# An encoder block's branch A: transposed probabilities kept for four tiles, values' products of 512 columns, gate projections dealt out by the tile's place in its four

## The chip, the cores and the metric

The kernel runs on one core of a Trainium2 chip. The metric is the device time of one execution in microseconds; before the change it is 1440.57 us, the median of 3 runs (1439.94 to 1441.64).

## What is computed

One block of an encoder over 1024 tokens and 16 meta tokens that are put ahead of them, width 1024. Two attentions run beside each other on the same normed input: branch A, a differential attention over all 1040 positions (4 heads of 2 x 64 for the scores, 128 wide values), and branch B, a windowed attention. Their outputs are gated, summed, projected, and a feed-forward block follows. Branch A, which the change is about, is cut from the reference:

```python
s1 = jnp.einsum('bqhd,bkhd->bhqk', q1, k1).astype(jnp.float32) * scale + bias
s2 = jnp.einsum('bqhd,bkhd->bhqk', q2, k2).astype(jnp.float32) * scale + bias
attn = jax.nn.softmax(s1, axis=-1) - lam * jax.nn.softmax(s2, axis=-1)
return jnp.einsum('bhqk,bkhe->bqhe', attn.astype(v.dtype), v)
...
y = rms_norm(y, subln_g) * (1.0 - lambda_init)
```

The gates are projections of the same input (`sigmoid(h @ W)` for each branch, 1024 columns each), needed only after both branches are done.

## The kernel before, in words

Float32 products are made of three products of split numbers (hi x hi, hi x lo, lo x hi), so most operands exist as a hi and a lo part: ACT copies the hi part, DVE or POOL subtracts it to get lo (`split`, L113 and L114).

The program runs in stages: projections for both branches with branch B (to about 320 us), then branch A's attention (to about 617 us), then the branches' projections `ppa` (L589, from 630.52 us), the gated merge, and the feed-forward block. The stage of branch A is the one that changes:

- It loops over 4 heads x 8 tiles of 128 query rows, `n` = 0 to 31, with a lag of one tile: in turn `n` the scores of tile `n` are made and tile `n`-1 is transposed. `t` is the tile's number in its head.
- **Scores** (`scores_a`, L645): for the two halves `m` = 1, 0, three chunks of 352, 352 and 336 keys, each two products into one PSUM bank `aps`. DVE reduces each chunk (L651), ACT takes the exponential of a half (L656), POOL scales half 1 (L659), DVE joins the halves (L662), POOL copies 32 columns (L663).
- **Transposes** (`transpose_a`, L674): 9 blocks of a tile in three parts (4, 4 and 1 blocks), each part into one bank `apt`; ACT writes the hi part (L677) and DVE the lo part (L678) into `at`. Banks of `aps`, `apt`, and the small `apst` and `apf` come from one pool of 5 ("sc"); a bank is taken again when DVE (or ACT) has read what was in it.
- **Values** (`values_a`, L687): for each pair of tiles 25 products of 256 columns, in three parts of 9, 9 and 7, into half of the bank `apy` (ring "acc", one bank).
- **Norm** (`normed_a`): after both pairs of a four ACT reads `apy` (L694, L696), PE sums squares (`apst`, L700) and spreads the factor over the partitions (`apf`, L708), DVE multiplies (`yg`, L709), and SP stores 512 columns to `ya_d` (L710).
- **Gate projections**: 256 steps of three 512-column products each (`pp_g`, L209), 8 steps for a chunk of 512 tokens; ACT copies the finished chunk (L596), SP stores it to `g_d` (L597). They don't depend on the attention, and are put between its products as filler by `fill`.

PE's order is written out by hand: a string `SLOTS` (L40; `SLOTS_LAST`, L41, for the last head) says for each tile in which order a chunk of scores (s), a gate step (g), a part of the transposes (t) and a step of what waits in `tail` (n: values, then the norm's steps) are issued. The other engines' orders are decided when the kernel is built. After the last tile the loop at L779 empties `tail`, with three gate steps behind each step, and `fill(1000)` issues what gates are left.

The next stage starts with loads that SP issues behind the last stores: two weights `first_w` (L581, into `m0`) and four tiles of branch B's output, each in two halves (L843, `yb_d0` to `yb_d3` into `m1`), which are then split by ACT and DVE (L113, L114) and read by `ppa`, nine products of `yb0`, `yb1`, `yb2` ahead of the first three of `yb3`.

## Time and profile before

| what | value |
|---|---|
| median of 3 runs | 1440.57 us (1439.94 to 1441.64) |
| the profiled execution | 1440.88 us, its span 1438.9 us |
| mean granted clock of TensorE | 0.998 |
| PE busy | 1424.8 us, 99% of the span |
| DVE busy | 907.1 us, 63% |
| ACT busy | 672.7 us, 47% |
| POOL busy | 469.7 us, 33% |
| branch A: first scores, last `apf`, first `ppa` | 322.47, 616.88, 630.52 us |

The time of an execution is its span and about 2 us around it. PE's matmuls are pipelined: a row of the timeline gives the start of a group and the time to the end of its last one, and the next group starts before that. What an instruction costs on PE is therefore the distance between starts; its duration is longer.

### The profile page before, as it was taken

The page shows a single profiled execution, that of the slowest core. Times are in us where ns is not written, and L with a number is a line of the kernel's source. Part 1 is how long each engine was busy: PE and PEld are TensorE (multiplying, and loading weights), DVE is VectorE, ACT ScalarE, POOL GpSimd, SP SyncE. Part 2 cuts the span into 40 slices and gives each one's busy share as a digit, 9 for nine tenths or more (in the row PEclk, how much of TensorE's full clock was granted, in tenths as well). Part 3 has the DMA queues.
Part 4 walks back from the last instruction along what each step waited for, and adds up shares of the span by engine and source line. Part 5 has one row for each costly group of instructions (what it writes and reads, how often), then busy time and mean ns, then how long its engine had stood idle before and what let it go on. Part 6 is the DMA issues. An engine that isn't in the chain of part 4 may idle for free.

```text
span 1438.9 us, 20909 instructions
## 1 busy us (share of the span) xinstructions
PE 1424.8 (99%) x7279; PEld 1222.8 (85%) x7279; DVE 907.1 (63%) x1806; ACT 672.7 (47%) x1275; POOL 469.7 (33%) x462
## 2 busy tenths in 40 slices
PE   8999999999999999999999999999999999999998
PEld 6988899988898989888888888888888888888886
DVE  7356566428686868546887966645445553787566
ACT  6355555425454545455345754333333333444444
POOL 5143233223323232211503045555445552000442
PEclk9999999999999999999999999999999999999999
DMA  7334433481524252078341633433323333954444
GB/s 233 87 97 124 116 101 88 112 247 53 155 75 148 75 153 69 30 271 270 123 148 74 189 104 125 153 111 107 105 96 97 109 102 103 340 201 139 124 125 147
DMA packets 159051, 191.68 MB, mean 133 GB/s; under 512 B 16113, under 2 KB 103601, under 8 KB 158945
## 3 DMA queue, kind: packets, MB, share of 16 engines
q1 hardware_dynamic: 158368, 189.28, 42.0%
q8 instruction: 58, 0.95, 0.3%
q10 hardware_dynamic: 576, 1.05, 0.2%
q14 instruction: 49, 0.39, 0.1%
HBM read 129.80 MB, written 53.94 MB: 128 GB/s over the span
## 4 chain that ended last, share of the span: by engine, by line
PE 93%; DVE 2%; DMA 2%; ACT 1%; issue 1%; POOL 1%; SPq 0%; DVEq 0%; ACTq 0%
PE pg L1266 29%; PE pd L1370 13%; PE pp_g L209 12%; PE aps L645 4%; PE po L1169 4%; PE apy L687 3%; PE pp_ka L209 3%; PE pp_va L209 3%; PE pp_qb L209 3%; PE pp_qa L209 3%; PE ppa L589 3%; PE apt L674 2%; PE bps L333 2%; PE po L1177 2%; PE bpy L373 1%; PE bpt L368 1%
## 5 line engine op out<-in xcount | busy, mean ns | idle before, releaser
L1266 PE MATMUL pg<-t,wop 128*128 128x512 f32 x1056 | 242.4, 389 | 0.0
L1266 PEld LDWEIGHTS pg<-t,wop 128*128 128x128 f32 x1056 | 198.3, 188 | 41.1
L1370 PE MATMUL pd<-ob,oa 128*128 128x512 f32 x924 | 210.1, 389 | 0.2 <-DVE ob L114 0.2
L114 POOL TENSOR_TENSOR wop<-wf,wop 128x512 fp32r<-128x512 f32 x114 | 154.4, 1355 | 162.5 <-ACT wop L113 148.8
L1370 PEld LDWEIGHTS pd<-ob,oa 128*128 128x128 f32 x924 | 173.4, 188 | 36.7 <-DVE ob L114 0.5
L1266 PE MATMUL pg<-b,wop 128*128 128x512 f32 x792 | 183.3, 389 | 0.8 <-ACT c L1278 0.8
L1266 PEld LDWEIGHTS pg<-b,wop 128*128 128x128 f32 x792 | 148.5, 188 | 31.7 <-ACT c L1278 1.0
L114 POOL TENSOR_TENSOR wl_c<-w_c,wh_c 128x1024 fp32r<-128x1024 f32 x32 | 78.3, 2447 | 123.6 <-ACT wh_c L113 97.0
L113 ACT ACTIVATE wop<-wf 128x512 fp32r<-128x512 f32 x128 | 80.7, 632 | 74.2 <-PE pg L1266 45.9
L656 ACT ACTIVATE as<-as,amn 128x1040 f32<-128x1040 f32 x64 | 74.5, 1165 | 73.6 <-DVE amn L651 73.6
L209 PE MATMUL pp_g<-hT_hi,wh_c 128*128 128x512 f32 x256 | 101.3, 396 | 0.0
L209 PE MATMUL pp_g<-hT_hi,wl_c 128*128 128x512 f32 x256 | 100.9, 394 | 0.0
L209 PE MATMUL pp_g<-hT_lo,wh_c 128*128 128x512 f32 x256 | 100.9, 394 | 0.0
L113 ACT ACTIVATE oa<-ra 128x512 fp32r<-128x512 f32 x77 | 48.7, 632 | 108.9 <-PE pd L1370 50.2
L645 PE MATMUL aps<-ak,aq 128*128 128x352 f32 (+1 forms) x384 | 92.7, 326 | 0.0
L114 POOL TENSOR_TENSOR oa<-ra,oa 128x512 fp32r<-128x512 f32 x27 | 35.0, 1296 | 169.3 <-ACT oa L113 167.9
L1043 DVE TENSOR_TENSOR s<-wf,wf 128x512 f32<-128x512 f32 x22 | 15.6, 707 | 114.4 <-DMA wf<-in_w_ff_up_dram 62.8
L645 PEld LDWEIGHTS aps<-ak,aq 128*128 128x128 f32 x384 | 69.5, 188 | 14.2 <-issue 0.2
L651 DVE CUSTOM_DVE_ANT_0 as<-aps,dist,amn 128x352 f32<-128x352 f32 (+1 forms) x128 | 71.3, 563 | 10.4 <-PE aps L645 8.3
L345 POOL TENSOR_SCALAR bs<-bs,bdn 128x432 f32<-128x432 f32 (+1 forms) x64 | 37.2, 602 | 122.8 <-DVE bdn L343 92.6
L651 DVE CUSTOM_DVE_ANT_0 as<-aps,dist,far_a 128x352 f32<-128x352 f32 x64 | 37.1, 580 | 43.2 <-PE aps L645 43.0
L659 POOL TENSOR_SCALAR as<-as,adn,neglam 128x1040 f32<-128x1040 f32 x32 | 39.0, 1219 | 75.6 <-DVE adn L657 75.6
(283 smaller groups left out, 3050.6 us busy)
## 6 DMA issues: line engine op xcount, KB each, us to landing
ra<-aop SPq DMA_DIRECT2D x77, 256.0 KB, 2.7
w_c<-in_w_in_dram SPq DMA_DIRECT2D x33, 512.0 KB, 3.9
wf<-in_w_ff_gate_dram SPq DMA_DIRECT2D x25, 512.0 KB, 3.9
wf<-in_w_ff_up_dram SPq DMA_DIRECT2D x25, 512.0 KB, 3.8
aop<-as SPq DMA_DIRECT2D x44, 256.0 KB, 2.1
aop<-c SPq DMA_DIRECT2D x33, 256.0 KB, 2.0
g_d<-gate_stage SPq DMA_DIRECT2D x32, 256.0 KB, 2.0
gt<-g_d SPq DMA_DIRECT2D x32, 256.0 KB, 4.1
```

Source lines behind the costliest of these rows:

```text
L113: nc.scalar.activation(hi, src, AF.Copy)
L114: lo_eng.tensor_tensor(lo, src, f32(hi), ALU.subtract)
L209: nc.tensor.matmul(ps[:, :n], a[:, c, :], b[:, c, at:at + n], start=(c == 0 and i == 0), stop=(c == DC - 1 and i == 2))
L589: nc.tensor.matmul(ps, w[:, a, j, :], src(j, b, tk), start=(j == 0 and n == 0), stop=(j == 3 and n == 2))
L645: nc.tensor.matmul(ps[:, :n], qs[m][:, t * P:(t + 1) * P], ks[m][:, vv, k0:k0 + n], start=(vv == 0), stop=(vv == 1))
L651: nc.vector.tensor_tensor_reduce(s[m][:, a:b], ps[:, a - k0:b - k0], far_by, slope, low, ALU.add, ALU.min, mn[:, m, i + j:i + j + 1])
L656: nc.scalar.activation(s[m][:, 0:L], s[m][:, 0:L], AF.Exp, bias=low, scale=-1.0, accum_out=dn[:, m:m + 1])
L659: (nc.gpsimd if t % 4 in COMBINE_POOL else nc.vector).tensor_scalar(s[1][:, 0:L], s[1][:, 0:L], dn[:, 1:2], neglam, ALU.mult, ALU.mult)
L687: nc.tensor.matmul(py[:, cols], v[:kp, a, k, :], at_[:kp, k, b, :], start=(k == 0 and j == 0), stop=(k == 8))
L1169: nc.tensor.matmul(sets_o[p][u], oa[:, a, u * P:(u + 1) * P], ob[:, b, :], start=(p in (1, 5) and j == 0 and k == 0), stop=(p in (2, 3) an ...
L1266: nc.tensor.matmul(ps, op[:, x, c, :], b[:, y, c, :], start=(p in (1, 5) and c == 0 and n == 0), stop=(p in (4, 2, 3) and c == 3 and n == ...
L1370: nc.tensor.matmul(ps[u], oa[:, a, u * P:(u + 1) * P], ob[:, b, :], start=(p in (1, 2, 5) and j == 0 and k == 0), stop=(p in (2, 3, 4) and ...
```

## The change

The transposed probabilities of four tiles are kept in three tiles (`at0` and `at1` with 4 blocks each, `at2` with one; 2, 1 and 2 buffers), so that the values of a four are 25 products of 512 columns, 200 in all instead of 400 of 256 columns. They are issued in six parts, blocks (4, 5), (6, 7), 0, 1, 2, (3, 8), where there were three parts for each pair, and only after all four tiles are transposed. The norm follows directly. And the slots differ by `n` % 4: 7, 3, 4 and 6 gate steps for tile 0, 1, 2, 3 of a four (5 for each before), 6, 2, 3 and 5 in the last head (4 before).

```diff
-SLOTS = "sgsgsngsgsgstntnt"
-SLOTS_LAST = "sgsgsngsgsstntnt"
+SLOTS = ("sggsgsgnsgsgsgstntnt", "sgsgssnsgstntnt", "sgsgsnsgsgstntnt", "sgsgsgnsgsgsgtntnt")
+SLOTS_LAST = ("sgsgsgnsgsgsgtntnt", "sgsssnsgstntnt", "sgsgsnsgsstntnt", "sgsgsnsgsgsgtntnt")
+VALUE_PARTS = ((4, 5), (6, 7), (0,), (1,), (2,), (3, 8))
...
-AT_BUFS = 2
+AT_BUFS = (2, 1, 2)
...
     def transpose_a(h, t, s, at_):
-        i = t % 2
+        i = t % 4
...
+            if i == 0:
+                at_.append(apool.tile([P, 4, 2, 512] if b < 2 else [P, 1, 1, 512], F32R, tag=f"at{b}",
+                                      name=f"at{b}_{h}_{t}", bufs=AT_BUFS[b]))
...
+    def values_a(v, at_, py):
+        first = True
+        for part in VALUE_PARTS:
+            for k in part:
+                for a, b in ((0, 0), (0, 1), (1, 0)) if k < 8 else ((0, 0),):
+                    nc.tensor.matmul(py, v[:, a, k, :], at_[k // 4][:, k % 4, b, :], start=first, stop=(k == 8))
+                    first = False
             yield
...
-        for what in SLOTS if n < 3 * NT else SLOTS_LAST:
+        for what in (SLOTS if n < 3 * NT else SLOTS_LAST)[n % 4]:
...
-        if n >= T_LAG and tiles[n - T_LAG][1] % 2:
+        if n >= T_LAG and tiles[n - T_LAG][1] % 4 == 3:
             tail.append(later(tiles[n - T_LAG]))
```

Lines behind the constants move down by two to six; instructions of branch A are now at L647 (`aps`), L680 (`apt`), L683 and L684 (hi and lo), L692 (`apy`), L713 (`apf`).

**Where a four begins to be used (head 1, turn of tile 5, the second of its four).** Names carry head, tile, half and first key of a chunk: `aps_1_5_1_704` is head 1, tile 5, half 1, keys from 704; `apt_1_3_1` is part 1 of tile 3's transposes. Before and after, the last transpose of tile 3 is followed by the chunk `aps_1_5_1_0` and a gate step. PE before, from the next chunk on:

```order
L645 MATMUL aps_1_5_1_352_4775<-ak1_1_4253,aq1_1_4252 128x352 x2
L209 MATMUL pp_g6_512_4727<-hT_hi_123,wh_c4096_4598 128x512
L209 MATMUL pp_g6_512_4727<-hT_lo_124,wh_c4096_4598 128x512
L209 MATMUL pp_g6_512_4727<-hT_hi_123,wl_c4096_4599 128x512
L645 MATMUL aps_1_5_1_704_4782<-ak1_1_4253,aq1_1_4252 128x336 x2
L687 MATMUL apy_1_1_4659<-at1_2_4497,av1_4264 128x256 x9
L209 MATMUL pp_g6_512_4727<-hT_hi_123,wh_c4096_4598 128x512
L209 MATMUL pp_g6_512_4727<-hT_lo_124,wh_c4096_4598 128x512
L209 MATMUL pp_g6_512_4727<-hT_hi_123,wl_c4096_4599 128x512
L645 MATMUL aps_1_5_0_0_4802<-ak1_0_4259,aq1_0_4258 128x352 x2
```

PE after, at the same place:

```order
L647 MATMUL aps_1_5_1_352_4707<-ak1_1_4213,aq1_1_4212 128x352 x2
L211 MATMUL pp_g6_512_4649<-hT_hi_123,wh_c4096_4547 128x512
L211 MATMUL pp_g6_512_4649<-hT_lo_124,wh_c4096_4547 128x512
L211 MATMUL pp_g6_512_4649<-hT_hi_123,wl_c4096_4548 128x512
L647 MATMUL aps_1_5_1_704_4714<-ak1_1_4213,aq1_1_4212 128x336 x2
L647 MATMUL aps_1_5_0_0_4722<-ak1_0_4219,aq1_0_4218 128x352 x2
L692 MATMUL apy_1_3_4726<-at1_1_0_4423,av1_4224 128x512 x6
L647 MATMUL aps_1_5_0_352_4733<-ak1_0_4219,aq1_0_4218 128x352 x2
```

Before, nine values' products on a pair (`at1_2` is that of head 1's tiles 2 and 3), a gate step and only then `aps_1_5_0_0` follow `aps_1_5_1_704`; now `aps_1_5_0_0` stands directly behind it, and the first six values' products of the four behind that.

DVE at this place before, from the lo part of the transposes' part 0 of tile 3 on (L678 is lo, L651 a chunk's reduction, L662 the join of the two halves of tile 4):

```order
L678 TENSOR_TENSOR at1_2_4497<-apt_1_3_0_4738,at1_2_4497 128x4x128
L651 ISA as1_1_5_4767,amn_1_5_4765<-aps_1_5_1_0_4768,dist_824,far_a_846 128x352
L651 ISA amn_1_5_4765 128x1
L657 RECIPROCAL adn_1_4_4677<-adn_1_4_4677 128x1
L678 TENSOR_TENSOR at1_2_4497<-apt_1_3_1_4752,at1_2_4497 128x4x128
L662 SCALAR_TENSOR_TENSOR as0_0_3464<-as0_0_3464,adn_1_4_4677,as1_1_4_4678 128x1040
L678 TENSOR_TENSOR at1_2_4497<-apt_1_3_2_4759,at1_2_4497 16x128
```

DVE after:

```order
L659 RECIPROCAL adn_1_4_4612<-adn_1_4_4612 128x1
L653 ISA as1_1_5_4699,amn_1_5_4697<-aps_1_5_1_0_4700,dist_824,far_a_846 128x352
L653 ISA amn_1_5_4697 128x1
L664 SCALAR_TENSOR_TENSOR as0_0_3464<-as0_0_3464,adn_1_4_4612,as1_1_4_4613 128x1040
L684 TENSOR_TENSOR at0_1_0_4409<-apt_1_3_0_4672,at0_1_0_4409 128x4x128
L684 TENSOR_TENSOR at1_1_0_4423<-apt_1_3_1_4686,at1_1_0_4423 128x4x128
```

The lo part of tile 3's part 0 stood ahead of the reduction of `aps_1_5_1_0` and of the join; now it stands behind both. In the built program `aps_1_5_0_0` waits now for that lo part, since it takes the bank of `apt_1_3_0`; before, it took the bank of `aps_1_5_1_0`.

**The end of branch A.** PE before, from the transposes of the last tile on (`apy_3_5` is the values' bank of the last four):

```order
L674 MATMUL apt_3_7_0_6607<-ident_99,as0_1_3465 128x128 x4
L687 MATMUL apy_3_5_6567<-at3_4_6233,av3_5838 128x256 x7
L674 MATMUL apt_3_7_1_6621<-ident_99,as0_1_3465 128x128 x4
L674 MATMUL apt_3_7_2_6628<-ident_99,as0_1_3465 128x128
L687 MATMUL apy_3_5_6567<-at3_6_6411,av3_5838 128x256 x9
L209 MATMUL pp_g13_512_6641<-hT_hi_123,wh_c2944_6502 128x512
```

PE after:

```order
L680 MATMUL apt_3_7_0_6421<-ident_99,as0_1_3465 128x128 x4
L713 MATMUL apf_3_0_6428<-ident_99,af_3_0_6383 128x128 x4
L680 MATMUL apt_3_7_1_6435<-ident_99,as0_1_3465 128x128 x4
L680 MATMUL apt_3_7_2_6442<-ident_99,as0_1_3465 128x128
L692 MATMUL apy_3_7_6446<-at1_3_4_6217,av3_5702 128x512 x6
L211 MATMUL pp_g13_512_6414<-hT_hi_123,wh_c2944_6327 128x512
```

Before, products for the pair before stood between the last tile's transposes, and the first products on the last pair read block 0; now the values of the whole four begin behind the last transpose, with blocks 4 and 5 (`at1`). Further on, 57 products `pp_g` (19 gate steps) stood between the last `apf` and the first `ppa`; now 24 (8 steps) do.

**SP's queue at the hand-off to the next stage.** Before, from the last store of `ya_d` on:

```order
L710 DMA ya_d3_94<-yg_3_1_6697 128x512
L597 DMA g_d14_89<-gate_stage_6763 128x512
L581 DMA m0_6856<-in_w_branch_b_dram 128x4x128 x2
L843 DMA m1_6857<-yb_d0_95 128x512 x2
L843 DMA m1_6857<-yb_d1_96 128x512 x2
L843 DMA m1_6857<-yb_d2_97 128x512 x2
L843 DMA m1_6857<-yb_d3_98 128x512 x2
L597 DMA g_d15_90<-gate_stage_6799 128x512
```

After, from the store ahead of it on:

```order
L599 DMA g_d15_90<-gate_stage_6598 128x512
L715 DMA ya_d3_94<-yg_3_1_6542 128x512
L583 DMA m0_6664<-in_w_branch_b_dram 128x4x128 x2
L844 DMA m1_6665<-yb_d0_95 128x512 x2
L844 DMA m1_6665<-yb_d1_96 128x512 x2
L844 DMA m1_6665<-yb_d2_97 128x512
L599 DMA g_d15_90<-gate_stage_6635 128x512
L844 DMA m1_6665<-yb_d2_97 128x512
L844 DMA m1_6665<-yb_d3_98 128x512 x2
```

Ahead of the two weights stood a gate store behind the `ya_d` store; now the `ya_d` store is the last ahead of them. The last gate chunk's store stood behind the eight loads of `yb_d`; it has moved ahead of the last three.

More of the change, by code (lines that the diff above doesn't have):

```diff
@@ L679, in transpose_a @@
             yield
-    def values_a(h, t, v, at_, py):
-        cols = slice(t % 4 // 2 * 256, t % 4 // 2 * 256 + 256)
-        for part in range(3):
-            for k in range(3 * part, 3 * part + 3):
-                kp = P
-                for j, (a, b) in enumerate(((0, 0), (0, 1), (1, 0)) if k < 8 else ((0, 0),)):
-                    nc.tensor.matmul(py[:, cols], v[:kp, a, k, :], at_[:kp, k, b, :],
-                                     start=(k == 0 and j == 0), stop=(k == 8))
+    def values_a(v, at_, py):
[5 more added lines that the diff above has]
+                    first = False
             yield
@@ L730, in later @@
         h, t, s, at_, v = done
-        if t % 4 == 1:
-            acc[0] = bank(psum2, "acc", f"apy_{h}_{t}", 1)
-        yield from values_a(h, t, v, at_, acc[0])
-        if t % 4 == 3:
-            yield from normed_a(h, t // 4, acc[0])
+        py = bank(psum2, "acc", f"apy_{h}_{t}", 1)
+        yield from values_a(v, at_, py)
+        yield from normed_a(h, t // 4, py)
     order_pe = tc.manual_schedule(engines={mybir.EngineType.PE})
@@ L755, in encoder_block @@
                 fill(G_HEAD if h else G_FIRST)
-            if t % 2 == 0:
-                at_ = apool.tile([P, 9, 2, 256], F32R, tag="at", name=f"at{h}_{t}", bufs=AT_BUFS)
+            if t % 4 == 0:
+                at_ = []
             s = [None, None]
```

5 lines of the change are left out of this document (2 added, 3 removed).

## The prediction

> **What bounds the kernel now.** I read the page's busy line and the chain of waits first, then the groups of lines in the stage of branch A, then its windows.
>
> ```profile
> PE 1424.8 (99%) x7279; PEld 1222.8 (85%) x7279; DVE 907.1 (63%) x1806; ACT 672.7 (47%) x1275; POOL 469.7 (33%) x462
> PE 93%; DVE 2%; DMA 2%; ACT 1%; issue 1%; POOL 1%; SPq 0%; DVEq 0%; ACTq 0%
> L209 PE MATMUL pp_g<-hT_hi,wh_c 128*128 128x512 f32 x256 | 101.3, 396 | 0.0
> ```
>
> PE is busy for 99% and makes 93% of the chain. So only two things change the time: fewer or cheaper products, and waits of PE that aren't there now. The groups (by form) and a window inside branch A:
>
> ```profile
> L687 PE MATMUL apy<-at,av 128*128 128x256 f32 x400 | 58.1, 288 | 0.0
> L651 DVE CUSTOM_DVE_ANT_0 as<-aps,dist,far_a 128x352 f32<-128x352 f32 x64 | 37.1, 580 | 43.2 <-PE aps L645 43.0
> ```
>
> ```profile
> 400.00:480.00 80.00, 80.00 (x494) 72.74 (x493) 60.92 (x201) 42.72 (x79) 23.05 (x25) 1.00 0.33 105
> ```
>
> PE works all 80 of 80 us at full clock, its values' products never idle ahead (0.0). DVE has 60.92 of 80 busy, and it is DVE that waits for PE's chunks (43.0). The stage is PE-bound, with DVE some 19 us of 80 behind the limit: enough on the average, not in every place.
>
> **The products.** The mean of 288 ns is no cost, since products overlap; the distance of starts is.
>
> ```profile
> 601.56 1.23 PE L687 MATMUL apy<-at,av 128*128 128x256 f32 x9
> 602.63 0.40 PE L209 MATMUL pp_g<-hT_hi,wh_c 128*128 128x512 f32 x1
> 617.55 0.39 PE L209 MATMUL pp_g<-hT_lo,wh_c 128*128 128x512 f32 x1
> 630.52 4.18 PE L589 MATMUL ppa<-yb,wbhb 128*128 128x512 f32 x17
> ```
>
> Nine products of 256 columns took 602.63 - 601.56 = 1.07 us, 119 ns each. From 617.55 to 630.52 stand 56 of the gates' products of 512 columns: 12.97 us, 232 ns each. So 400 x 0.119 = 47.6 us become 200 x 0.232 = 46.3: **-1.3 us**. Halving the count saves almost nothing, because a product costs by its columns. I bound the term by 0 and -2.6.
>
> **Where a four begins.** Gate steps are only moved (20 for four tiles before and after), so PE's work stays; but where there are fewer, PE comes earlier to things that others make. In the turn of the second tile of a four, `aps_0_0` now stands right behind `aps_1_704`, takes the bank of the first transposes of the tile before, and waits for their lo part, which DVE now does behind the join (the order of DVE in the section above). Before, at the place shown there:
>
> ```profile
> 426.56 0.47 PE L645 MATMUL aps<-ak,aq 128*128 128x336 f32 x2
> 426.87 0.60 PE L674 MATMUL apt<-ident,as 128*128 128x128 f32 x4
> 427.34 0.55 DVE L651 CUSTOM_DVE_ANT_0 as<-aps,dist,amn 128x320 f32<-128x320 f32 x1
> 428.00 1.16 ACT L656 ACTIVATE as<-as,amn 128x1040 f32<-128x1040 f32 x1
> 428.13 0.71 PE L674 MATMUL apt<-ident,as 128*128 128x128 f32 x5
> 428.60 0.57 PE L645 MATMUL aps<-ak,aq 128*128 128x352 f32 x2
> 429.06 0.19 ACT L656 ACTIVATION_READ_ACCUMULATOR as<-as,amn 128x1 f32 x1
> 429.20 0.58 DVE L651 CUSTOM_DVE_ANT_0 as<-aps,dist,far_a 128x352 f32<-128x352 f32 x1 [0.38 <-PE aps L645]
> 429.79 0.68 DVE L678 TENSOR_TENSOR at<-apt,at 128x512 fp32r<-128x512 f32 x1
> 430.38 1.29 DVE L662 SCALAR_TENSOR_TENSOR as<-as,adn,as 128x1040 f32<-128x1040 f32 x1
> 431.02 1.22 PE L687 MATMUL apy<-at,av 128*128 128x256 f32 x9
> ```
>
> ```profile
> 590.32 0.60 PE L708 MATMUL apf<-ident,af 128*128 128x128 f32 x4
> 590.76 0.60 PE L674 MATMUL apt<-ident,as 128*128 128x128 f32 x4
> ```
>
> Count from the start of tile 4's last chunk (426.56). DVE's side: the chunk is reduced by 427.89 (+1.33), the exponential and its sum end at 429.25 (+2.69); then a reciprocal and the reduction of `aps_1_5_1_0` (0.58), which now stand in front, so about 430.0; the join to 431.25; the lo part, 0.68, to about 431.9: **+5.35**. PE's side: the chunk 0.31 (426.56 to 426.87), a gate step 0.70 (three times 0.232), four transposes, `apf` and four transposes more at 0.44 each (590.32 to 590.76) with the single one (428.13 to 428.60 holds five in 0.47) 1.35, then the three chunks with two gate steps between (428.60 to 431.02) 2.42: **+4.78**. PE waits about 0.6 us. The values' products behind it read the second transposes' lo part, which DVE ends 0.6 us later, while PE has 0.33 us of chunk and one product on the hi part: 0 to 0.3 more. I take 0.7 for each, with bounds 0.5 and 1.0. Seven turns are of this kind (two in each head, but the first has no values and stands below). In the two of the last head one gate step less stands in front: 0.7 more each. 7 x 0.7 + 2 x 0.7 = **+6.3** (4.9 to 8.4). The other cover is gone too: before, nine products and a gate step, 1.07 + 0.70, lay between.
>
> **The start.** Tiles 1 and 2 of the first head get 3 and 4 gate steps instead of 5 and 5, and have no values to do.
>
> ```profile
> 330.38 0.23 DVE L651 CUSTOM_DVE_ANT_0 as<-aps,no_dist,amn 128x16 f32<-128x16 f32 x1 [0.40 <-PE aps L645]
> 332.91 0.47 PE L645 MATMUL aps<-ak,aq 128*128 128x336 f32 x2
> 337.48 1.30 DVE L662 SCALAR_TENSOR_TENSOR as<-as,adn,as 128x1040 f32<-128x1040 f32 x1
> 339.69 1.14 PE L674 MATMUL apt<-ident,as 128*128 128x128 f32 x9
> ```
>
> The join of tile 1 ends at 338.78 and its transposes start at 339.69, a margin of 0.7 behind POOL's copy of 0.2. DVE's last wait for PE is that of 0.40 at 330.38; behind it DVE sets the pace. PE would come three gate steps, 2.1 us, earlier: 2.1 - 0.7 = 1.4 if DVE gains those 0.40 too, 2.1 if the first chunks come later by the two steps more in tile 0. **+1.7** (0 to 2.1).
>
> **The end.** The last four's values now begin with blocks 4 and 5, the transposes just done.
>
> ```profile
> 597.65 0.71 PE L674 MATMUL apt<-ident,as 128*128 128x128 f32 x5
> 598.12 1.50 PE L687 MATMUL apy<-at,av 128*128 128x256 f32 x9
> 598.29 0.77 ACT L677 ACTIVATE at<-apt 128x512 fp32r<-128x512 f32 x2 [0.67 <-PE apt L674]
> 598.92 0.88 DVE L678 TENSOR_TENSOR at<-apt,at 128x512 fp32r<-128x512 f32 x2 [0.58 <-ACT at L677]
> 599.46 0.40 PE L209 MATMUL pp_g<-hT_hi,wh_c 128*128 128x512 f32 x1
> ```
>
> Before, the nine products took 1.34 instead of 1.07 (a wait of 0.27 for block 0's parts). Now the first needs ACT's hi part (598.29 + 0.6), 0.8 after 598.12, and the second DVE's lo part (598.92 + 0.69, about 599.65), 0.5 more: 1.3 - 0.27 = **+1.0** (0.8 to 1.3).
>
> **The hand-off.** The six parts take more filler between them, so 8 gate steps instead of 19 are left between the last `apf` and `ppa`. What must happen in that time hangs on `apf`:
>
> ```profile
> 616.88 0.60 PE L708 MATMUL apf<-ident,af 128*128 128x128 f32 x4
> 618.29 0.32 SPq L710 DMA_DIRECT2D ya_d<-yg  x1
> 620.67 1.02 SPq L581 DMA_DIRECT2D m<-in_w_branch_b_dram  x2
> 621.74 4.60 SPq L843 DMA_DIRECT2D m<-yb_d  x8
> 631.39 1.38 DVE L114 TENSOR_TENSOR yb<-m,yb 128x512 fp32r<-128x512 f32 x2
> ```
>
> ```profile
> DMA to landing us min/median/max: 4.3/5.1/6.2
> ```
>
> SP goes in order: `ya_d`'s store waits for `yg`, the weights' and `yb_d`'s loads stand behind it. The lo part that `ppa` needs for `yb3` was ready at 631.39 + 1.38 = 632.77, which is 15.9 us after `apf`, and PE came to it nine products behind 630.52, at 632.6 to 632.8: there is no margin even now. After the change the weights start at 618.29 + 0.38 - 616.88 = 1.8 after `apf` instead of 3.8, since the gate store between is gone; the same spacing puts the lo part at 15.9 - 2.0 = 13.9. PE is there after 0.44 + 24 x 0.232 + 9 x 0.232 = 8.1 to 8.3. **+5.6 us.** The last gate chunk's store now stands ahead of the last three loads and waits for ACT's copy of PE's last gate product, 6.0 + 0.8 after `apf`; so `yb3`'s first load is issued near 7.9, and with a landing of 4.3 to 6.2 and 0.63 and 0.69 for hi and lo the wait is 5.3 to 7.2. If the landing is quicker because less runs beside it, and the store comes no later than the loads, 4.0. So 4.0 to 7.2. Nothing gives it back: the products behind are as many as before.
>
> `at1`'s single buffer costs nothing: blocks 4 to 7 are used in the first two parts, ahead of the next four's second transposes. The values' bank is read by ACT three tiles before it is taken again.
>
> **Sum**: against the profiled execution, -1.3 + 6.3 + 1.7 + 1.0 + 5.6 = +13.3 on 1440.9: **1454.2 us**. The profiled execution is 0.3 us above the median of the runs, inside their spread.
>
> **Rivals.**
> (1) PE's clock falls in the hand-off's wait, where PE works some 2.1 of 8 us.
>
> ```profile
> 5.86:9.27 3.41, 1.02 (x5) 0.29 (x4) 2.61 (x4) 1.78 (x5) 1.59 (x3) 1.00 1.08 344
> 9.27:12.68 3.41, 3.41 (x12) 2.31 (x13) 2.89 (x4) 2.98 (x4) 3.09 (x2) 0.50 1.09 342
> ```
>
> At the start of the program a window of 3.41 us with 1.02 busy was followed by one at clock 0.50. The same here would lose half of 3.41 us: 1454.2 + 1.7 = 1455.9. For it: the wait's share of work is as low. Against: the wait comes in pieces with products between. The Trainium skill ("TensorE: Matmul & The Clock Gate", Part 1: The HAM clock gate) lets the clock fall only after a whole idle window of about 3.4 us; by that rule this rival gives nothing and the sum stays, but the row above, with 1.02 us of work in the window, speaks against so sharp a bound.
> (2) Only the hand-off costs: DVE, which waits for PE in total 43 us, catches up and the stage has no new waits: 1440.9 - 1.3 + 5.6 = 1445.2. It holds if DVE ends the lo part 0.6 us sooner than I count.
> (3) Only the stage costs, and the loads are started earlier than the queue says: 1440.9 - 1.3 + 9.0 = 1448.6.
> (4) Faster: the 256-column products are bound by their weight loads and not by their columns, so half of the loads are saved. The page has 85% busy for weight loads, 188 ns each. Were 188 ns the distance of starts, 400 x 0.188 - 200 x 0.232 = 28.8 us would go: 1440.9 - 28.8 + 14.6 = 1426.7. It outweighs the waits' 14.6 us from a distance of (46.4 + 14.6) / 400 = 0.153 us on; the row shows 0.119.
> (5) The change doesn't do what it says, for instance because wider products need more distance than the gates' ones: with 0.238 nothing is saved, and the waits stay: 1455.5.
>
> **How the numbers follow.** The forecast 0.63, rival 1 0.13, rival 2 0.08, rival 3 0.08, rival 4 0.03, rival 5 0.02, and 0.03 that both groups of waits are hidden (1439.6). Ends of the forecast: 1440.9 - 2.6 + 4.9 + 0 + 0.8 + 4.0 = 1448.0, and 1440.9 + 8.4 + 2.1 + 1.3 + 7.2 = 1459.9. Not all ends meet, so with rival 3 inside I take 1447.0 to 1459.5; rivals 2 and 4 stay out. A measurement here tells 0.2%, 2.9 us, from no change: faster 0.04, same 0.05, slower 0.91.
>
> **What would show it.** Right: idle time ahead of `aps` and `apy` released by DVE's lo part and ACT, in each second tile of a four; a distance of 0.232 between values' products; 4 to 7 us idle ahead of `ppa`, released by ACT and DVE on `yb`. Wrong: no idle ahead of `aps`, `ppa` 6 us behind `apf` without a wait, or values' products at another distance.

## The result, and the profile after

The kernel before took 1440.26 us (median of four runs, 1439.75 to 1441.64), the changed kernel 1459.42 us (median of four, 1454.82 to 1461.69). The ratio is 1.0121, with an interval of 1.0110 to 1.0133: slower by 19 us. The profiled execution of the changed kernel took 1457.47 us with a span of 1455.6, so what its trace shows explains 16.6 us against the profiled execution before (1440.88). The rest lies in the spread of its runs, now 6.9 us wide where it was 1.9. One execution among those of the experiments, of R2, took 1774 us at a mean granted clock of 0.752 and is left out of every number below.

The busy line of the page, and then four groups by form, first the chunks of the kernel before, then three of the changed kernel in the window of branch A (322.6 to 640 us). The columns of a group are busy time, mean ns of one, and idle time of PE ahead of it with what ended it.

```profile
PE 1428.7 (98%) x7079; PEld 1213.1 (83%) x7079; DVE 909.2 (62%) x1806; ACT 673.7 (46%) x1275; POOL 464.9 (32%) x462
```

```profile
L645 PE MATMUL aps<-ak,aq 128*128 128x352 f32 x256 | 64.2, 332 | 0.0
...
L647 PE MATMUL aps<-ak,aq 128*128 128x352 f32 x256 | 64.7, 334 | 3.4 <-DVE at L684 2.6 <-DVE amn L653 0.6
L692 PE MATMUL apy<-at,av 128*128 128x512 f32 x200 | 57.8, 410 | 3.0 <-DVE at L684 2.4 <-ACT at L683 0.6
L680 PE MATMUL apt<-ident,as 128*128 128x128 f32 x288 | 43.8, 273 | 1.5 <-DVE amn L653 1.5
```

The values' products are 200 now and not 400, as the edit says; their idle time is no longer 0.0 but 3.0, and the chunks, which had 0.0 too, now wait 2.6 us for DVE's lo parts. PE's busy time is 3.9 us higher than before although it has 200 instructions fewer. Busy time is no measure of the saving: the mean of a values' product went from 288 to 410 ns with twice the columns, and how much that is in time only the distances of starts tell (below).

From the list of PE's waits (us in total, how many, the longest), the two ahead of `ppa`:

```profile
PE ppa L591 <- ACT yb L115: 1.8, 1, 1.8
PE ppa L591 <- DVE yb L116: 1.1, 2, 0.9
```

The waits of the groups and these stand at the places that the prediction named. The milestones of PE say how much each stretch took; a stretch ends at the start of its last product, `apf`'s with the last of its four transposes. Steps of gates (0.695 us each) that moved across a border are taken out: 19 stood between the last `apf` and the first `ppa` before, 8 now, so 11 x 0.695 = 7.65 us of branch A's time are only moved.

| stretch | before us | after us | moved steps | cost us |
|---|---|---|---|---|
| start to the first `aps` | 322.47 | 324.64 | 0 | +2.2 |
| first `aps` to the last `apf` | 294.74 | 311.98 | -7.65 | +9.6 |
| last `apf` to the end of `ppa` | 13.32 + 87.48 | 7.63 + 90.82 | +7.65 | +5.3 |
| `ppa` to the end | 720.92 | 720.53 | 0 | -0.4 |
| sum | 1438.9 | 1455.6 | | +16.7 |

**Where a four begins.** The timeline of PE and DVE at one such place (start, time until the last one of the row ends, engine; idle time ahead in brackets):

```profile
434.45 1.29 DVE L664 SCALAR_TENSOR_TENSOR as<-as,adn,as 128x1040 f32<-128x1040 f32 x1
435.66 1.28 DVE L684 TENSOR_TENSOR at<-apt,at 128x512 fp32r<-128x512 f32 x2
...
435.44 0.47 PE L647 MATMUL aps<-ak,aq 128*128 128x336 f32 x2
436.40 0.59 PE L647 MATMUL aps<-ak,aq 128*128 128x352 f32 x2 [0.49 <-DVE at L684]
```

The join (L664) runs until 435.74, the first lo part (L684) behind it until about 436.3, and `aps_1_5_0_0`, the first chunk of the same tile's half 0, which takes that bank, starts at 436.40 with an idle time of 0.49. PE's starts tell a little more than the brackets, since a bracket counts from a modelled end: against the distance that the same instructions keep where they don't wait, 0.65 us is lost here. In the seven turns the loss by starts is 1.35 (362.09 and 363.29), 0.65 (403.05), 0.65 (this one), 0.66 (476.71), none, 1.35 (548.94) and 1.85 (581.31): 6.5 us.

**The start and the end.** PE's transposes of the second tile, then the last four's values:

```profile
343.11 1.06 PE L680 MATMUL apt<-ident,as 128*128 128x128 f32 x8 [1.46 <-DVE amn L653]
...
607.95 0.49 PE L692 MATMUL apy<-at,av 128*128 128x512 f32 x1 [0.58 <-ACT at L683]
608.80 1.42 PE L692 MATMUL apy<-at,av 128*128 128x512 f32 x5 [0.36 <-DVE at L684]
```

By starts the first costs 1.62, with 0.30 ahead of a chunk at 336.70: 1.9. The end costs 0.74 + 0.62 = 1.36, where 0.16 was lost before.

**The hand-off.** SP's queue, a row of ACT, then PE and DVE, and then three windows of 3.41 us (busy time of PE, PEld, DVE, ACT and POOL, then the granted clock, the DMA engines' share and GB/s):

```profile
637.70 0.32 SPq L715 DMA_DIRECT2D ya_d<-yg  x1
638.11 1.03 SPq L583 DMA_DIRECT2D m<-in_w_branch_b_dram  x2
639.20 2.39 SPq L844 DMA_DIRECT2D m<-yb_d  x5
643.17 0.32 SPq L599 DMA_DIRECT2D g_d<-gate_stage  x1
643.54 1.39 SPq L844 DMA_DIRECT2D m<-yb_d  x3
...
647.72 1.40 ACT L115 ACTIVATE yb<-m 128x512 fp32r<-128x512 f32 x2 [0.72 <-DMA m<-yb_d]
...
644.25 0.50 PE L591 MATMUL ppa<-yb,wbhb 128*128 128x512 f32 x1 [1.77 <-ACT yb L115]
645.63 0.96 PE L591 MATMUL ppa<-yb,wbhb 128*128 128x512 f32 x3 [0.88 <-DVE yb L116]
...
648.38 1.47 DVE L116 TENSOR_TENSOR yb<-m,yb 128x512 fp32r<-128x512 f32 x2 [0.40 <-ACT yb L115]
```

```profile
643.11:646.52 3.41, 1.39 (x4) 0.67 (x4) 2.29 (x3) 3.11 (x7) 1.56 (x2) 1.00 0.98 348
646.52:649.93 3.41, 3.17 (x8) 1.73 (x7) 2.85 (x5) 1.98 (x4) 0.00 (x0) 0.50 1.02 328
649.93:653.35 3.42, 3.42 (x16) 2.85 (x16) 1.38 (x2) 3.39 (x6) 0.00 (x0) 1.00 1.05 387
```

The weights start at 638.11, 1.8 us behind the last `apf` (636.29 is the start of its four transposes). The last gate store does stand between the fifth load and the last three: SP is done with the fifth at 641.59 and with the store at 643.49. ACT waits for the sixth load until 647.72, 11.4 us behind the last `apf`. `ppa` waits 1.77 for the first tile's hi part and 0.88 for a lo part; then it runs at half clock for one window. `yb3`'s lo part ends at 648.38 + 1.47 = 649.85, 13.6 us behind the start of `apf`, and its product starts at 649.90, 0.49 late by starts.

### The profile page after: what moved, and what is told of

It reads as the page before. It is cut to its first block, busy times and chain, and to the rows that moved or that the text cites. A ratio compares the mean times of both kernels' runs of the same rounds, so it can differ in the third digit from the quotient of the medians.

```text
span 1455.6 us, 20484 instructions
## 1 busy us (share of the span) xinstructions
PE 1428.7 (98%) x7079; PEld 1213.1 (83%) x7079; DVE 909.2 (62%) x1806; ACT 673.7 (46%) x1275; POOL 464.9 (32%) x462
## 5 line engine op out<-in xcount | busy, mean ns | idle before, releaser
L116 POOL TENSOR_TENSOR wop<-wf,wop 128x512 fp32r<-128x512 f32 x114 | 151.4, 1328 | 164.4 <-ACT wop L115 154.5
L647 PE MATMUL aps<-ak,aq 128*128 128x352 f32 (+1 forms) x384 | 93.2, 328 | 3.4 <-DVE at L684 2.6
L647 PEld LDWEIGHTS aps<-ak,aq 128*128 128x128 f32 x384 | 69.0, 188 | 19.6 <-DVE at L684 3.8
L653 DVE CUSTOM_DVE_ANT_0 as<-aps,dist,amn 128x320 f32<-128x320 f32 (+1 forms) x128 | 70.9, 564 | 12.1 <-PE aps L647 10.3
L115 ACT ACTIVATE wh_c<-w_c 128x1024 fp32r<-128x1024 f32 x33 | 35.0, 1061 | 58.5 <-PE pp_g L211 32.6
```

The source lines that it names most:

```text
L115: nc.scalar.activation(hi, src, AF.Copy)
L116: lo_eng.tensor_tensor(lo, src, f32(hi), ALU.subtract)
L647: nc.tensor.matmul(ps[:, :n], qs[m][:, t * P:(t + 1) * P], ks[m][:, vv, k0:k0 + n], start=(vv == 0), stop=(vv == 1))
L653: nc.vector.tensor_tensor_reduce(s[m][:, a:b], ps[:, a - k0:b - k0], far_by, slope, low, ALU.add, ALU.min, mn[:, m, i + j:i + j + 1])
```

## Experiments

Theory 1, the prediction's: the loss is made of waits of PE, in the stage where PE comes sooner than DVE's lo parts and join, and in the hand-off where `yb_d`'s loads hang on the last `apf`. They are independent and add up. Rivals: the clock makes the hand-off's loss; or the wide products with their buffers cost by themselves, and the places of the gate steps only move it. Unless said otherwise the edit is to the changed kernel. In the tables "stage" is from the first `aps` to the last `apf` and "hand-off" from there to the end of `ppa`, both with moved steps taken out as above and against before's 294.74 and 87.60 us (13.32 + 87.48 less 19 steps).

**E1: the steps given back to the hand-off.**

```
     while tail:
         step_tail()
-        fill(3)
+        fill(2)
```

> The changed kernel with two gate steps instead of three behind each step of the tail, so that 18 gate steps instead of 8 stand between the last apf and the first ppa (19 before the change). Theory 1 (the hand-off is a wait for the yb loads, which start from apf, and the idle PE then loses its clock): the 3.5 us of waits ahead of and in the first ppa and the half clock of 3.4 us there (1.7 us of work) both go, the stage's waits of about 10 us stay: 5 us faster than the changed kernel, near 1453 to 1454 us. Rival (the loads are late for another reason, for instance contention with the gate stores): the wait ahead of ppa stays at 2 us or more, and the time within 2 us of the changed kernel's.

Measured 1450.95 us beside 1442.56, ratio 1.0062 (1.0045 to 1.0079). 18 gate steps stand ahead of `ppa` again.

```profile
639.64 0.40 PE L211 MATMUL pp_g<-hT_hi,wl_c 128*128 128x512 f32 x1
639.87 2.47 PE L591 MATMUL ppa<-yb,wbhb 128*128 128x512 f32 x10
```

`ppa` starts 0.23 behind the last gate product, the spacing of two products without a wait. There is no half clock near it, and the hand-off costs 12.62 + 87.52 - 18 x 0.695 = 87.63, nothing against 87.60. The stage keeps its +9.4. So the hand-off's cost hangs on these steps alone, and the two groups add up. The median is lower than the 1453 to 1454 expected: of the 8.0 us between the two profiled executions (1455.60 and 1447.63) 5.3 are the hand-off's, and 2.2 lie ahead of the first `aps`, where this edit moves nothing.

**E2: the old places of the gate steps, with the four-tile values.**

```
-SLOTS = ("sggsgsgnsgsgsgstntnt", "sgsgssnsgstntnt", "sgsgsnsgsgstntnt", "sgsgsgnsgsgsgtntnt")
-SLOTS_LAST = ("sgsgsgnsgsgsgtntnt", "sgsssnsgstntnt", "sgsgsnsgsstntnt", "sgsgsnsgsgsgtntnt")
+SLOTS = ("sgsgsngsgsgstntnt",) * 4
+SLOTS_LAST = ("sgsgsngsgsstntnt",) * 4
```

> The changed kernel with the slots of before for every tile (5 gate steps each, 4 in the last head): values of 512 columns and four-tile buffers stay. Theory 1 (the wait where a four begins comes from reading values right behind the last transposes; the slots only choose which product pays): the waits on aps in each second tile go, and apy waits there instead, for DVE's lo part of the second transposes, 1.5 to 2 us in at least half of the fours; the start's 1.9 us go. Hand-off as in the changed kernel. Time within 4 us of the changed kernel's, 1454 to 1460. Rival (the new slots alone are at fault, the grouping of values is free): no new waits in the stage, 1448 us or less.

Measured 1461.25, ratio 1.0130 (1.0115 to 1.0145). Its stage costs 313.82 - 9 x 0.695 - 294.74 = +12.8. The waits:

```profile
PE apy L692 <- DVE at L684: 4.9, 4, 1.6
PE ppa L591 <- ACT yb L115: 2.1, 1, 2.1
PE aps L647 <- DMA ak<-ka_d: 2.0, 3, 1.0
```

The waits on lo parts go from the chunks to the values and are longer; the chunks now wait for the keys' loads. Two transposes wait too, one of them (at 351.11) 1.45 us by starts for POOL's copy of 32 columns, a wait that R1 meets again. The time is 1.3 us above the range that was expected, and the rival, no new waits, is refuted. The four-tile values want another place for the gate steps than the old one, so the edit to the table is no mere extra: it takes back 3.2 us of 12.8.

**E3: the new places of the gate steps alone, in the kernel before.**

```
-SLOTS = "sgsgsngsgsgstntnt"
-SLOTS_LAST = "sgsgsngsgsstntnt"
+SLOTS = ("sggsgsgnsgsgsgstntnt", "sgsgssnsgstntnt", "sgsgsnsgsgstntnt", "sgsgsgnsgsgsgtntnt")
+SLOTS_LAST = ("sgsgsgnsgsgsgtntnt", "sgsssnsgstntnt", "sgsgsnsgsstntnt", "sgsgsnsgsgsgtntnt")
...
-        for what in SLOTS if n < 3 * NT else SLOTS_LAST:
+        for what in (SLOTS if n < 3 * NT else SLOTS_LAST)[n % 4]:
```

> The kernel before with the new slots alone; values stay 256 columns wide for each pair. Theory 1: the start's 1.9 us wait is that of the changed kernel, since neither has values there; at each second tile of a four the wait is smaller than the changed kernel's, 0.2 to 0.9 us, since PE does not go on to values of tiles just transposed; the hand-off has its old cover of 19 gate steps and no wait. Sum 5 to 8 us: 1445 to 1449 us. Rival (the waits belong to the grouping of values alone): at most the start's 1.9 us, 1442 us or less.

Measured 1451.06 beside 1442.56, ratio 1.0059 (1.0044 to 1.0074). The stage costs 304.38 - 2 x 0.695 - 294.74 = +8.3, and the hand-off with 17 steps 11.92 + 88.47 - 17 x 0.695 - 87.60 = +1.0.

```profile
PE apt L674 <- DVE amn L651: 1.5, 1, 1.5
PE aps L645 <- DVE amn L651: 1.0, 2, 0.5
PE aps L645 <- DVE at L678: 0.8, 1, 0.8
```

The wait at the start is there with its full 1.62 us, with the values of two tiles and in the kernel before: it comes from the places alone, as the prediction had it. Those in the fours are other ones (0.28 in four turns, 1.00 in one, 1.27 in each of the last head's two), so there the places and the values work together. In sum it was more than the 5 to 8 us expected, and the rival, that the grouping of the values alone brings the waits, falls.

**E4: is it the clock?** 17 transposes into an unused bank, behind the last gate step, keep PE at work while it waits. They add work whose result nothing reads.

```
     fill(1000)
+    warm = pp_bank("warm")
+    for _ in range(17):
+        nc.tensor.transpose(warm[:, 0:P], ident, ident)
```

> The changed kernel with 17 transposes of the identity (109 ns each, 1.85 us) between the last gate product and ppa, written to a spare bank that nobody reads: PE works in the first 1.9 us of the hand-off's wait. Theory 1 (part of the hand-off's cost is the clock, which falls because PE is idle): the clock stays at 1.00 behind it and the 1.7 us of lost work go; the wait for yb itself ends at the same moment as before. 1 to 2 us faster than the changed kernel, less spread between runs. Rival (the clock does not matter or falls all the same): same time or up to 1 us slower.

Measured 1459.34, ratio 1.0121 (1.0106 to 1.0137): the changed kernel's time. The timeline and the windows over the hand-off:

```profile
643.06 2.02 PE L788 MATMUL warm<-ident 128*128 128x128 f32 x17
...
650.40 0.50 PE L591 MATMUL ppa<-yb,wbhb 128*128 128x512 f32 x1 [0.79 <-ACT yb L115]
651.13 2.11 PE L591 MATMUL ppa<-yb,wbhb 128*128 128x512 f32 x8 [0.22 <-DVE yb L116]
```

```profile
643.40:646.80 3.40, 2.58 (x19) 1.92 (x17) 1.83 (x2) 2.83 (x6) 2.10 (x2) 1.00 1.02 387
646.80:650.20 3.40, 2.37 (x8) 0.97 (x6) 2.70 (x5) 2.31 (x4) 0.00 (x0) 1.00 0.95 322
```

The clock stays at 1.00 through the whole hand-off, and it still costs 7.87 + 91.08 - 8 x 0.695 - 87.60 = +5.8. The 1 to 2 us that I expected from the clock didn't come; the rival held. The last wait, for `yb3`'s lo part, ends at 651.13, 14.1 us behind the start of this run's last `apf` (637.03); in the changed kernel it was 649.90 - 636.29 = 13.6. These 0.5 us are the difference of the two costs, 5.8 and 5.3. So the one window of half clock in the changed kernel, which ended at 649.93, lay beneath a wait that the loads set. The loads and their splits are the cause, and the clock isn't, as long as it is one window that ends ahead of them.

**R0: the changed kernel again, unaltered, to see how it varies.**

> The changed kernel once more, unaltered, to see which parts of its time return in another execution. Theory 1 (fixed waits in the stage and at the hand-off, and a part at the program's start that depends on where the clock's windows fall): the waits in branch A return at the same places within 0.1 us each, 9.6 us in sum, and the hand-off costs 5 to 6 us again; the first scores start at 322 to 323 us in an execution without a second half-clock window before 25 us, at 324 to 326 us in one with it. Rival (the times differ because waits on DMA differ): the hand-off's wait differs by 2 us or more between the two profiles.

Measured 1457.69 (1455.81 to 1459.12), ratio 1.0111 (1.0095 to 1.0127). Each wait in the stage agrees within 0.03 us with those of the first trace; the stage is 311.87 against 311.98. The hand-off isn't the same:

```profile
639.33:642.74 3.41, 1.30 (x5) 0.50 (x3) 0.78 (x1) 2.93 (x6) 2.25 (x2) 1.00 1.05 387
642.74:646.15 3.41, 2.56 (x6) 1.90 (x7) 3.20 (x5) 1.63 (x3) 0.24 (x1) 0.50 0.96 321
646.15:649.56 3.41, 2.47 (x5) 1.24 (x5) 1.97 (x3) 2.55 (x4) 0.00 (x0) 0.50 1.03 384
649.56:652.98 3.42, 3.42 (x9) 2.64 (x8) 0.71 (x2) 3.41 (x7) 0.00 (x0) 0.50 1.04 347
```

Three windows at half clock instead of one, and the hand-off costs 7.72 + 94.10 - 8 x 0.695 - 87.60 = +8.7, where 5 to 6 were expected. In the last of them PE is busy throughout, and so it loses half the window, 1.7 us, half of the 3.4 us that this execution lost beyond the first. The other half isn't the clock: the wait itself is longer. ACT's row at the sixth load, and PE's first product on `yb3`'s lo part:

```profile
646.89 1.94 ACT L115 ACTIVATE yb<-m 128x512 fp32r<-128x512 f32 x3 [2.43 <-DMA m<-yb_d]
...
649.03 0.79 PE L591 MATMUL ppa<-yb,wbhb 128*128 128x512 f32 x1
```

The sixth load lets ACT go on 646.89 - 633.93 = 13.0 us behind the start of this run's last `apf`, and not 11.4 as in the changed kernel, and that product starts at 649.03, 15.1 us behind `apf` instead of 13.6. So 1.5 us are a later load, and 1.9 are work at half clock behind the end of the wait (649.03 to 652.98). The windows also lie otherwise against the wait here (642.74 is 8.5 us behind the start of `apf`'s last transpose at 634.26, 646.52 was 9.9 behind 636.62). Which of the two differences, the phase or the longer wait, made three windows of one, two executions can't tell.

**E5: other places for the gate steps in the fours**, without the chunk right behind `aps_1_704` in the second tile.

```
+SLOTS = ("sggsgsgnsgsgsstgntnt", "sgsgsgssnstntnt", "sgsgsnsgsgstntnt", "sgsgsgnsgsgsgtntnt")
+SLOTS_LAST = ("sggsgsgnsggsgstntnt", "sgsgsgssnstntnt", "sgsgsnsgsstntnt", "sgsgsnsgsstntnt")
```

> The changed kernel with other slots for the first and second tile of a four (a gate step between the first and second transposes of the first, a gate step more ahead of the half-0 chunks and values one chunk later in the second); in the last head 7, 3, 3, 3 gate steps instead of 6, 2, 3, 5. First four, tail and hand-off as in the changed kernel. Theory 1 (PE waits there for DVE's lo part by 0.65 to 1.85 us, since too little stands between; the place of one gate step decides): of the 6.5 us of waits of the fours at most 1 is left, 5.5 to 6.5 us faster than the changed kernel. Rival (DVE has no time to spare in the stage, so the waits move elsewhere): 2 us faster or less, with waits at other chunks or transposes.

Measured 1453.58 beside 1441.79, ratio 1.0084 (1.0071 to 1.0098).

```profile
PE ppa L591 <- ACT yb L115: 2.8, 2, 2.3
```

No chunk waits any more. Of the fours' 6.5 us 0.18 are left; the start's 1.62 + 0.30 and the end's 0.74 + 0.62 stand as they were. The stage costs 305.40 - 12 x 0.695 - 294.74 = +2.3. The hand-off costs +7.4. It has two windows of half clock (637.70 to 644.50), but they aren't all of the 2.1 us more than in the changed kernel: one gate step fewer, 0.7 us, stands ahead of `ppa`, and `yb3`'s lo part is ready 642.78 + 0.69 - 628.93 = 14.5 us behind the last `apf`, 1.0 later.

**R1: all three places mended.** E5's table, the old places for the first four tiles, the last four's values begun with blocks 0 and 1, and two steps of filler for three in the tail (with two ahead of it).

```
+SLOTS_FIRST = ("sgsgsngsgsgstntnt", "sgssngsgsgsgtntnt", "sgsgsngsgsgstntnt", "sgsgsngsgsgstntnt")
+PARTS_LAST = ((0, 1), (2, 3), (4, 5), (6, 7, 8))
...
+    fill(2)
     while tail:
         step_tail()
-        fill(3)
+        fill(2)
```

> The slots of the run e5_fours, the slots of before for the first four tiles (one of them rearranged), the last four's values in the order of the blocks with two gate steps ahead, and two gate steps instead of three in the tail, so that 19 or so are left for the hand-off. Theory 1 (the change's whole cost is these four waits; the 512-column products themselves save about 1 us): all waits of 0.3 us and more in branch A go, none ahead of ppa, and the time is 0.5 to 2.5 us below that of the kernel before. Rival (something else in the change costs, for instance the wider products or DVE's other order): 3 us or more above the kernel before.

Measured 1443.77 beside 1441.79, eleven and fifteen runs, ratio 1.0013 (1.0004 to 1.0022). The 0.5 to 2.5 us below the kernel before that I expected didn't come. The profiled execution, the fastest of the eleven, has a span of 1438.94, that of before to 0.02 us. Hand-off -0.1, stage +0.2: all waits of the changed kernel are gone, and one that the changed kernel hadn't is there (E2 had it), with POOL's instructions ahead of it:

```profile
348.19 0.33 PE L682 MATMUL apt<-ident,as 128*128 128x128 f32 x1 [1.28 <-POOL as L667]
...
344.54 3.44 POOL L118 TENSOR_TENSOR wl_c<-w_c,wh_c 128x1024 fp32r<-128x1024 f32 x1 [2.56 <-ACT wh_c L117]
347.93 0.20 POOL L667 COPY as<-as 128x32 f32<-128x32 f32 x1
```

In the kernel before the same copy of 0.21 us ran at 345.60, ahead of the split of the gates' weights, which followed at 345.90. Now the split stands in front with 3.44 us, and the third tile's last transpose waits 1.44 us by starts.

**R2: the split moved away from the copy** by two gate steps fewer ahead of the first head.

```
-G_FIRST = 30
+G_FIRST = 28
```

> The run r1_all with 28 instead of 30 gate steps ahead of the first scores, so that on POOL the split of the next gate weights (3.4 us there) no longer stands between tile 2's join and its copy of 32 columns, for which PE waited 1.44 us in r1_all. Theory 1 (this wait is all that kept r1_all from being faster; its values' products took 48.8 us from start to start and the kernel before's 50.3): that wait goes, no other of 0.3 us or more comes, and the span of the profiled execution is 1 to 2 us below 1438.9. Rival (the gain of the products is lost somewhere outside branch A, or between executions): the median is not below that of the kernel before.

Measured 1447.51 (1446.41 to 1450.18, five runs) beside 1441.87, ratio 1.0046 (1.0033 to 1.0059). That wait is gone and the stage takes 293.56, 1.18 less than before. But the two steps stand ahead of `ppa` now (21), where PE waits for the weights' parts `wbhb` (1.30 for ACT and 0.80 for POOL): the hand-off costs 14.70 + 89.69 - 21 x 0.695 - 87.60 = +2.2. What was saved at one place came back as a wait at another, which I hadn't expected; why these parts come too late there I didn't follow up.

**R3: the copy on DVE instead.**

```
-        nc.gpsimd.tensor_copy(
+        (nc.vector if (h, t) == (0, 2) else nc.gpsimd).tensor_copy(
```

> The run r1_all with the copy of 32 columns of the first head's tile 2 on DVE instead of POOL, all other orders on PE, ACT and SP as in r1_all. Theory 1 (in r1_all PE waited 1.44 us for this copy, which stood behind the split of gate weights on POOL; the products save 1.2 to 1.5 us): the wait shrinks to 0.3 us or less, branch A from the first scores to the last apf takes about 293.6 us instead of 294.9 (294.7 in the kernel before), the hand-off stays at the kernel before's, and the median is 0.5 to 1.5 us below the kernel before's where no window of half clock is added. Rival (r1_all's median, 2.0 us above the kernel before with the same span in its profile, has another cause, in the executions and not in branch A): the stage is faster by 1.1 us as said, and the median is still 0 to 2 us above.

Measured 1444.10, ratio 1.0011 (1.0002 to 1.0020), and the wait is still there, 1.43 us:

```profile
349.22 1.38 DVE L667 COPY as<-as 128x32 f32<-128x32 f32 x1
347.11 3.44 POOL L118 TENSOR_TENSOR wl_c<-w_c,wh_c 128x1024 fp32r<-128x1024 f32 x1 [2.55 <-ACT wh_c L117]
```

My expectation failed: the queue on POOL wasn't the whole reason. DVE's copy of 32 columns took 1.38 us and ended at 350.60, with POOL's split (347.11 + 3.44 = 350.55). On another engine it seems still to have waited for that instruction. The Trainium skill ("SBUF — State Buffer", SBUF: two separate sides) gives DVE and GpSimd one port pair, held for a whole instruction while the other blocks, where the DVE instruction is in a two-port mode or has two SBUF inputs; the two ends, 0.05 us apart, agree with it, but in which mode this copy ran no row shows.

**R4: the copy on ACT.**

```
+        if (h, t) == (0, 2):
+            nc.scalar.copy(tail_out, tail_in)
+        else:
+            nc.gpsimd.tensor_copy(tail_out, tail_in)
```

> The run r1_all with the copy of 32 columns of the first head's tile 2 on ACT, where nothing runs beside POOL's split (in r3_copy, on DVE, the copy took 1.38 us and ended only when POOL's split of 3.44 us did). Theory 1 (the wait of 1.43 us in r1_all and r3_copy is that copy beside that split): the wait goes, branch A from the first scores to the last apf takes 293.4 to 293.8 us (294.7 in the kernel before), the hand-off stays. Median: r1_all and r3_copy stood 2 us above the kernel before, so about 0.5 us above it now, and at most 1.5 us above. Rival (DVE or PE meet the next wait right behind it): 294.5 us or more.

Measured 1441.94 beside 1442.07, eleven and fifteen runs, ratio 1.0004 (0.9994 to 1.0013). A row of its timeline, and its group of values' products:

```profile
345.71 0.22 ACT L670 COPY as<-as 128x32 f32<-128x32 f32 x1 [0.86 <-DVE as L666]
```

```profile
L698 PE MATMUL apy<-at,av 128*128 128x512 f32 x200 | 56.3, 406 | 0.0
```

The copy takes 0.22 us, while the split runs on POOL from 344.46 to 347.93, the wait is gone, and the values' products never idle ahead. The stage takes 293.47 us, 1.27 less than before, and the span is 1438.2. This is the change without its waits. It brings 1.3 us in the stage and, in the time, no difference from the kernel before that can be measured; it doesn't beat it.

**B: the kernel before, run again**, for its own variation.

> The kernel before once more, for a second profile of its start: where the half-clock windows fall before 25 us, and when the first scores start. Theory 1 (the second window at the start is a matter of the execution and not of the change): the start of the first scores lies anywhere from 322.3 to 325.5 us, with the later times in executions with a second window. Rival (the kernel before never has it): 322.5 us and one window only.

Measured 1443.02, span 1440.99. Its stage (294.69) and its 19 steps (13.32) are those of the first trace to 0.05 us, but `ppa` took 91.03 us instead of 87.48:

```profile
695.34:698.75 3.41, 1.60 (x8) 1.02 (x7) 3.41 (x5) 0.63 (x1) 1.66 (x1) 1.00 0.22 71
698.75:702.16 3.41, 3.41 (x10) 2.64 (x9) 3.38 (x5) 1.38 (x3) 1.67 (x1) 0.50 0.12 45
```

PE waited 1.81 us for a part of `wbha`, had 1.60 of work in that window, and ran the next at half clock. So the kernel before also loses a few us in some executions, and a single time of either kernel says little under 3 us.

## Why the prediction was right, and by how much it was short

The forecast was slower by 13.3 us, 1454.2 with a range to 1459.5. The runs' median is 1459.42, inside the range by 0.08 us, which is luck: R0, the same kernel, had 1457.69, and two of the first four runs lie above the range. The profiled execution compares with the one that the sum was made against at +16.6. The waits stood where the prediction had them, and the sum was short by 3.3 us; most of that, 2.2 us, lies at the start of the program, where no term stood. Term by term:

- **The products, -1.3.** Measured -1.27, in R4, where nothing else is left. By starts the 200 products of R1 and R4 take 48.8 us and the 400 of before 50.3, -1.5. The median distance there is 232 ns for 512 columns and 120 for 256, which the prediction had from other rows as 232 and 119. Rival 4, the weight loads as the bound, needed 153 and falls.
- **Where a four begins, +6.3.** Measured +6.5, in seven turns of 0 to 1.35 in the earlier heads and 1.35 and 1.85 in the last, where 0.7 and 1.4 were predicted. One turn lost nothing, which the mean hides. E5 takes 6.3 of it away by places alone.
- **The start, +1.7.** Measured 1.9, at the named transposes; E3 shows it without the four-tile values.
- **The end, +1.0.** Measured 1.36 - 0.16 = +1.2.
- **The stage together, +7.7.** Measured +9.6. The four terms give -1.3 + 6.5 + 1.9 + 1.2 = 8.3; 1.3 us are in waits too small to be told apart in the list. Here the sum was too small because it counted only the places that I had priced.
- **The hand-off, +5.6.** With the clock kept up, E4 gives +5.8; `yb3`'s lo part let PE go on 13.6 us behind the last `apf` in the changed kernel and 14.1 in E4, where 13.9 stood. The picture was a little wrong: the wait comes in pieces from the first `yb` on, and not as one at `yb3`. So the sign that I had named, 4 to 7 us idle ahead of `ppa`, didn't show: the list has 1.8 + 1.1 = 2.9 us; by starts 5.2 us are lost, the rest of them in and around products at half clock beneath the same wait. The end of the wait is near the predicted one and so is the price, in this execution; R0's +8.7 lies above the term's range of 4.0 to 7.2, 1.9 of it by the clock. E1 takes all of it away.
- **Rival 1, the clock.** It got a chance of 0.13 and one window, +1.7. It happened in each trace with a hand-off of 7 to 10 gate steps (the changed kernel, R0, E2, E5), apart from E4. The first window cost nothing, as it lay beneath the wait (+5.3 with one window, +5.8 with none). What I missed is that the half clock can go on behind the wait's end, as in R0, where it cost 1.9 us beside the 1.5 of a later load. So it was under-weighted in its chance, and its size in these traces is 0 to 1.9.
- **What no term had.** 2.2 us ahead of the first `aps`, where the change moves nothing. The traces show half clock that begins 15 to 19.3 us into the program in the changed kernel, E2, E4, E5, R2 and R3; in before, B, E1, E3, R1 and R4 it begins at 8.5 to 9.6 us alone, and R0 (the same kernel as the changed one) has none. The first `aps` starts at 323.86 to 325.51 in the former (R2's with two gate steps fewer ahead) and at 322.19 to 323.36 in the latter, so the late half clock goes with 1.4 to 3.0 us beside before's 322.47. Since the same kernel stands on both sides, it is a matter of the execution, though neither trace of the kernel before has it. Why an execution gets it stays open.

Rivals 2 and 3, that only one group costs, are both refuted by E1 and E5, where one group is taken away and the other stays. Rival 5, that wider products need more distance, falls by R4.

What isn't settled: the profiled execution is one of four, and the median of the changed kernel is 2 us above it. A hand-off like R0's (+8.7 instead of +5.3 for the same kernel) would do that, but only two of its executions have a trace. Half clock alone doesn't explain it: the slowest of the four runs, 1461.69, had a mean clock of 0.996, above the profiled execution's 0.995. The 1.3 us of small waits in the stage aren't told apart either.

## What to carry to other kernels

Where one engine is busy for 98% and another follows with a margin of half a microsecond, filler between the steps isn't idle time to be dealt out freely: each piece stands in front of a certain wait, and a table of places has to be read against the engine that makes the data. Products that cost by their columns don't get cheaper by being fewer, so a change that halves their number should be priced by the distance of starts before anything is rearranged for it. And work taken from ahead of a hand-off comes back as a wait when the loads behind the hand-off hang on the same event: E1 needed one number to undo 5.3 us.

## What the runs showed of the hardware

The clock fell with much less idle time than a whole window. Windows at full clock with 1.30, 1.39, 1.44 and 1.60 us of PE's work in 3.41 were each followed by one at 0.50, and so was one with 1.91 (E2); windows with 2.35 and more (E4's 2.58 and 2.37) were not. A window at half clock with 2.08, 2.47 or 2.56 us of work was followed by another, and one with 3.17 by full clock. The amount of work doesn't decide alone: of E4's two windows with 1.49 us the one from 4.94 was followed by full clock and the one from 11.76 by half, and R0's with 1.61 (14.69 to 18.10) by full clock. The first pair of the changed kernel, at the start of the program, then E4's window from 4.94 with the one behind it, and E2's, behind which the clock was 0.50:

```profile
11.63:15.05 3.42, 1.44 (x11) 1.00 (x9) 3.42 (x4) 3.20 (x5) 1.74 (x1) 1.00 0.92 259
15.05:18.46 3.41, 2.08 (x9) 2.09 (x10) 3.06 (x6) 1.50 (x4) 2.48 (x4) 0.50 0.80 233
...
4.94:8.35 3.41, 1.49 (x7) 0.49 (x5) 1.73 (x3) 2.11 (x3) 1.20 (x2) 1.00 1.01 315
8.35:11.76 3.41, 2.43 (x15) 1.51 (x15) 2.93 (x3) 2.99 (x6) 3.04 (x3) 1.00 1.14 357
...
647.35:650.77 3.42, 1.91 (x5) 0.85 (x6) 2.26 (x4) 3.19 (x6) 1.08 (x1) 1.00 1.04 377
```

The Trainium skill ("TensorE: Matmul & The Clock Gate", Part 1: The HAM clock gate) asks for a whole idle window for the fall and lets the windows run freely, so that the same kernel varies by their phase. The second part agrees with the traces, where the first half clock of the start begins anywhere from 8.5 to 17.0 us into the program; the first doesn't, since none of these windows was idle and the clock fell behind 1.30 to 1.91 us of work in it. Between 1.49 and 1.91 us both outcomes occur, and what decides there no run shows.

The other thing is R3's copy: 1.38 us on DVE for 32 columns beside a split on POOL, and 0.22 on ACT in R4 beside the same split. That split itself took 3.44 us in R1 and R3, where the kernel before had it in 2.41 at 345.90; in both it began within 0.1 us of the join on DVE (L666, at 344.47 in R1 and 347.03 in R3). That one held up the other is argued and not tested.
